# Where eleven parameter rows and five small weight loads stand in one load queue

## The chip, the cores and the metric

The kernel runs on one core of one Trainium2 chip. The time is device microseconds (us) of one execution; lower is better. A core has five engines with a queue each, and every queue is worked through in order: TensorE (PE, matrix products and transposes; PEld is its weight load), VectorE (DVE), ScalarE (ACT), GpSimd (POOL) and SyncE (SP). SP computes nothing here: it issues the transfers between HBM and the on-chip memory.

## The reference, cut to what matters

One decoder layer for 1024 prompt tokens and 64 new sample tokens (8 sequences of 8). The part around the change is the head of the layer:

```python
def rmsnorm(x, g):
    y = xf * lax.rsqrt(jnp.mean(xf * xf, axis=-1, keepdims=True) + RMS_EPS)
    return (y * g).astype(x.dtype)
...
h = rmsnorm(x, lw['g_mix'])
proj = h @ lw['w_in']                                   # 1024 x 3328
...
xs = proj + (prev - proj) * lw['mu_shift']              # token shift
r, k, v, dw, da, dg = jnp.split(xs, cuts, axis=-1)
w_log = -jax.nn.softplus(-(lw['w0'] + jnp.tanh(dw) @ lw['w2'])) - 0.5
decay = jnp.exp(-jnp.exp(w_log))
a = jax.nn.sigmoid(lw['a0'] + da @ lw['a2'])
g = jax.nn.sigmoid(dg) @ lw['g2']
```

Behind it come a recurrence over 1024 tokens (RWKV-7), a short convolution, stick-breaking attention over the prompt and over a paged cache, an output projection, a squared-ReLU MLP and a gated embedding. All of it is float32. The parameters `mu_shift`, `w0`, `a0`, `k_k`, `k_a`, `r_k`, `gn_w`, `gn_b`, `conv_w`, `g_mlp` and `g_ple` are vectors of 256 to 1024 numbers; `w2`, `a2` and `g2` are matrices of 64, 64 and 128 rows by 256.

## The kernel before

**Head of the kernel.** The 1088 tokens are nine tiles of `x`: eight of 128 rows and one of 64 rows (the sample tokens). `x_tile(i)` (L107 to L111) takes one of four buffers `xt` (`bufs=4`) and loads 128 rows of 1024 floats, 512 KB, with one transfer on SP (L110). Tile 4 therefore needs the buffer of tile 0, tile 5 that of tile 1, and so on. `gbc` (L116) is `g_mix` repeated on all partitions.

The loop over nine tiles (L181 to L202) does this for each: ACT squares the row and sums it (L189) and takes the root (L190); DVE takes the reciprocal (L192) and multiplies tile, reciprocal and `gbc` into `h` (L193), which is the last reader of the tile's buffer; PE transposes `h` in eight blocks (L198) into two of five PSUM banks that `tr()` hands out in turn; ACT copies each bank to a rounded half `h_hi` (L200) and DVE forms the remainder `h_lo` (L201). Each product of the kernel is then three matmuls: high by high, low by high, high by low.

**Weights.** `Weights.load` (L147 to L160) reads 512 KB into one of two buffers `wr` (L156), ACT rounds it to `wh` (L158), POOL forms the remainder `wl` (L159). The first one, `w_da`, is the 256 columns of `w_in` for decay, rate and gate: two transfers.

**Parameter rows.** Behind the loop, the eleven vectors are loaded as 44 rows of 128 floats into one tile `prow`, one SP transfer each (L213); PE transposes `prow` (L218), DVE copies it to `par` (L219) and forms `om`, which is one minus `mu_shift` (L221) and one minus `k_a` (L222). The transpose takes the next bank of `tr()`.

**Small weights.** `wl2` holds `w2`, `a2` and `g2`: five SP transfers (L300 to L302), 64 KB each and 128 KB for `g2`. ACT rounds it (L303), POOL forms the remainder (L304). `lora` (L344 to L353, its matmuls at L349) uses them. Then comes `sh`, the 8 rows of `state_shift` (L308), which PE transposes (L311).

**First projection.** `rw_tile` (L319 to L342) multiplies 128 columns of a weight with `h` in three chunks of 384, 384 and 320 tokens (`gemm_t`, L169 to L171), into three banks `acc()` in turn. ACT copies each bank out twice: `raw` (L330, L332) and `xs` scaled by `om` (L333); DVE adds the shifted `raw` scaled by `mu_shift` (L334). The fourth chunk needs the first bank back, and so `om`.

**What sets the order.** The program is traced in the order above, and a planner then writes each engine's queue: it steps through a model of the machine, and whenever an engine is free it gives it the earliest traced instruction that is ready in the model. So a load whose buffer isn't free yet is overtaken by later loads that need nothing. `tc.issue_after(ins)` forbids this for the instructions of its block on `ins`'s engine: they come behind `ins` in that queue. It is an order of issue only, no wait for `ins` to finish.

Of the kernel before, what the change touches and what calls it, by code (L numbers as in the profile page):

```python
# [48 lines left out]
def hybrid_step(ctx: ExitStack, tc: tile.TileContext, I, O):  # L49
    nc = tc.nc  # L50
    V, S, G, PE, SP = nc.vector, nc.scalar, nc.gpsimd, nc.tensor, nc.sync
# [46 lines left out]
    xp_in = I["x_prompt"][0]  # L98
    xs_in = I["x_sample"].rearrange("b j d -> (b j) d")
# [7 lines left out]
    def x_tile(i):  # L107
        r = 128 if i < 8 else NS
        xt = xpool.tile([128, D], F32, name="xt", bufs=4)
        SP.dma_start(xt[:r], xp_in[i * 128:i * 128 + 128, :] if i < 8 else xs_in)  # L110
        return xt, r  # L111

    xts = [x_tile(0)]
    gbc = xpool.tile([128, D], F32, name="gbc")
    gm = I["g_mix"]
    SP.dma_start(gbc, bass.AP(tensor=gm.tensor, offset=gm.offset, ap=[[0, 128], [1, D]]))  # L116
    xts += [x_tile(i) for i in range(1, 3)]


# [61 lines left out]
    for i in range(9):  # L181
        if i == 1:
            w_da = w_cols(768)
        if i + 3 < 9:
            xts.append(x_tile(i + 3))
        xt, r = xts[i]
        st = xpool.tile([128, 2], F32, name="st", bufs=5)
        h = xpool.tile([128, D], F32, name="h", bufs=3)
        S.activation(h[:r], xt[:r], AF.Square, accum_out=st[:r, 0:1])  # L189
        S.activation(st[:r, 1:2], st[:r, 0:1], AF.Sqrt, bias=eps_rms[:r], scale=1.0 / D)  # L190
        rs = xpool.tile([128, 1], F32, name="rs", bufs=5)
        V.reciprocal(rs[:r], st[:r, 1:2])  # L192
        V.scalar_tensor_tensor(h[:r], xt[:r], rs[:r], gbc[:r], op0=ALU.mult, op1=ALU.mult)  # L193
        for g in range(2):
            pt = tr().rearrange("p (k t) -> p k t", k=4)
            for k in range(4):
                c = (4 * g + k) * 128
                PE.transpose(pt[:, k, :r], h[:r, c:c + 128], ident[:r, :r])  # L198
            dst = slice(i * 128, i * 128 + r)
            S.copy(hT[0][g][:, :, dst], pt[:, :, :r])  # L200
            V.tensor_sub(hT[1][g][:, :, dst], pt[:, :, :r], f(hT[0][g][:, :, dst]))  # L201
# [6 lines left out]
    prow = consts.tile([nrows, 128], F32)  # L208
    col = {}
    at = 0  # L210
    for name, n in rows:
        src = I[name]
        SP.dma_start(prow[at:at + n, :], bass.AP(tensor=src.tensor, offset=src.offset, ap=[[128, n], [1, 128]]))  # L213
        col[name] = at
        at += n
    par = consts.tile([128, nrows], F32)
# [76 lines left out]
    def pe_tile(name, dtype=F32):  # L293
        return rp.tile([128, LW], dtype, name=name, tag="pe", bufs=12)


    wl2, wl2h, wl2l = (pe_tile(f"wl2{i}", d)[:, :768].rearrange("p (i c) -> p i c", i=3) for i, d in
                       enumerate((F32, F32R, F32R)))
    for s in range(2):
        SP.dma_start(wl2[64 * s:64 * s + 64, 0], I["w2"][0])  # L300
        SP.dma_start(wl2[64 * s:64 * s + 64, 1], I["a2"][0])
    SP.dma_start(wl2[:, 2], I["g2"][0])  # L302
    S.copy(wl2h, wl2)  # L303
    G.tensor_sub(wl2l, wl2, f(wl2h))  # L304
    shT = rp.tile([128, 8, NB], F32, name="shT")
# [71 lines left out]
    for j in range(2):  # L377
# [14 lines left out]
        for a in range(2):  # L392
            rb = pe_tile("rb", F32R)
            rbs.append((rb, rp.tile([128, 2, 64], F32R, name=f"rb8{a}")))
            for d, i0, i1 in ((rb[:, :1024], 0, 8), (rbs[a][1].rearrange("p s d -> p (s d)"), 8, 9)):
                d = d.rearrange("p (i s d) -> p i s d", i=i1 - i0, s=2)
                src = rk[:, i0:i1, :, None].to_broadcast([128, i1 - i0, 2, 64])
# [5 lines left out]
        for t0, n in CH:  # L403
            ps = tr()
            for t in range(t0, t0 + n, 128):
                r = min(128, T - t)
# [361 lines left out]
    ap = tc.alloc_tile_pool(name="att_a", bufs=1, side="right", reuse_waits="tile")  # L768
# [6 lines left out]
    for n, name in enumerate(("q_gain", "k_gain")):  # L775
        src = I[name]
# [761 lines left out]
    ap = tc.alloc_tile_pool(name="att_b", bufs=1, side="right", reuse_waits="tile")  # L1538
# [213 lines left out]
```

## Time and profile before

| | |
|---|---|
| time, median of 3 runs | 1705.01 us (1703.33 to 1708.07) |
| the profiled execution | 1706.69 us; its span, first to last instruction, 1705.1 us; so 1.6 us lie around the span |
| mean granted TensorE clock | 0.987 |
| PE busy | 1637.8 us, 96% |
| PEld / DVE / ACT / POOL busy | 87% / 65% / 48% / 43% |
| DMA | 202.26 MB, mean 119 GB/s |

In the profile each instruction has a start in us from the beginning of the span, a length, an engine (`SPq` is SP's queue, with the time that an issue took), the line in the kernel, the operation, what it writes and reads, and in square brackets how long its engine was idle before it and which instruction or transfer ended that. The word "issue" there means that the profile shows nothing waited for. The view by windows gives busy time of each engine in stretches of the span, the granted clock, the DMA engines' busy share and GB/s.

### The profile page before, as it was taken

Reading aid. Unit: us, or ns where it says so; the run is one execution under the profiler, and the core shown is the slowest. Engines: PE = TensorE matmul, PEld = TensorE weight load, DVE = VectorE, ACT = ScalarE, POOL = GpSimd, SP = SyncE. Lnnn points to the kernel's source line nnn. Section 1 sums busy time; section 2 is a strip of 40 time slices with the busy share of each in tenths; the row PEclk is TensorE's granted clock in tenths of the full one; section 3 lists DMA queues with packets and bytes.
Section 4 is the critical chain, followed back from the end, with each engine's and each line's share of the span. In section 5 each row is a group of like instructions: output and inputs, shape, how many; then the busy total and the mean of one; then the engine's idle time right before and its main releaser. Section 6 shows DMA issues by size and latency. Waiting matters only on the chain.

```text
span 1705.1 us, 30847 instructions
## 1 busy us (share of the span) xinstructions
PE 1637.8 (96%) x11853; PEld 1476.2 (87%) x11853; DVE 1105.0 (65%) x1918; ACT 820.7 (48%) x1627; POOL 727.3 (43%) x778
## 2 busy tenths in 40 slices
PE   6999899999899889999999999999999999999898
PEld 5899888889898767888887778987999999999698
DVE  6266844555277759888854345378777777764986
ACT  6633433343343657666543444364444334436753
POOL 4123121123232664443434654366655445538621
PEclk9999999999999999999999999999999999999999
DMA  5134466325523763433245665322322222323232
GB/s 189 49 120 124 142 166 178 72 78 158 160 66 96 226 170 124 137 121 116 78 121 149 187 178 189 112 84 77 97 90 87 87 87 90 98 76 105 87 120 56
DMA packets 212372, 202.26 MB, mean 119 GB/s; under 512 B 58305, under 2 KB 177761, under 8 KB 212098
## 3 DMA queue, kind: packets, MB, share of 16 engines
q1 hardware_dynamic: 202498, 179.33, 35.4%
q0 software_dynamic: 5120, 16.78, 3.3%
q10 hardware_dynamic: 4608, 4.20, 1.0%
q8 instruction: 93, 1.52, 0.4%
q14 instruction: 53, 0.43, 0.1%
HBM read 163.27 MB, written 36.98 MB: 117 GB/s over the span
## 4 chain that ended last, share of the span: by engine, by line
PE 76%; DVE 10%; DMA 6%; ACT 3%; issue 3%; SPq 2%; POOL 1%; ACTq 0%; DVEq 0%; POOLq 0%
PE b L1094 12%; PE b L1096 11%; PE b L1095 11%; PE b L1453 4%; PE b L1455 4%; PE b L1454 4%; PE b L169 3%; PE b L170 3%; PE b L171 3%; PE b L797 2%; PE b L795 2%; PE b L796 2%; PE b L942 2%; DMA wr<-in_w_in 1%; PE b L512 1%
## 5 line engine op out<-in xcount | busy, mean ns | idle before, releaser
L1075 POOL TENSOR_TENSOR wl<-wr,wh 128x512 fp32r<-128x512 f32 x182 | 255.1, 1411 | 265.5 <-ACT wh L1074 226.3
L1074 ACT CAST wh<-wr 128x512 fp32r<-128x512 f32 x308 | 187.9, 621 | 308.9 <-PE b L1095 198.0
L1522 DVE TENSOR_TENSOR x<-b,x 128x288 f32<-128x288 f32 (+1 forms) x384 | 199.2, 528 | 97.2 <-PE b L1096 86.0
L1094 PE MATMUL b<-ah,wh 128*128 128x288 f32 (+1 forms) x768 | 253.7, 331 | 3.2 <-DVE x L1522 2.1
L1096 PE MATMUL b<-ah,wl 128*128 128x288 f32 (+1 forms) x768 | 252.2, 328 | 0.0
L1095 PE MATMUL b<-al,wh 128*128 128x288 f32 (+1 forms) x768 | 252.0, 328 | 0.0
L1094 PEld LDWEIGHTS b<-ah,wh 128*128 128x128 f32 x768 | 144.5, 188 | 15.3 <-DVE x L1522 4.8
L1096 PEld LDWEIGHTS b<-ah,wl 128*128 128x128 f32 x768 | 144.5, 188 | 10.2
L1095 PEld LDWEIGHTS b<-al,wh 128*128 128x128 f32 x768 | 144.6, 188 | 9.3 <-DVE al L1426 0.3
L1094 PE MATMUL b<-nh,wh 128*128 128x512 f32 x320 | 129.1, 403 | 5.4 <-DVE x L1413 3.3
L795 PE MATMUL b<-wh,h_hi 128*128 128x256 f32 x432 | 127.4, 295 | 5.1 <-ACT sq L805 5.1
L1095 PE MATMUL b<-nl,wh 128*128 128x512 f32 x320 | 128.1, 400 | 0.0
L1096 PE MATMUL b<-nh,wl 128*128 128x512 f32 x320 | 127.7, 400 | 0.0
L797 PE MATMUL b<-wh,h_lo 128*128 128x256 f32 x432 | 126.8, 293 | 0.0
L796 PE MATMUL b<-wl,h_hi 128*128 128x256 f32 x432 | 124.7, 289 | 0.0
L1075 DVE TENSOR_TENSOR wl<-wr,wh 128x512 fp32r<-128x512 f32 x126 | 102.4, 815 | 26.4 <-ACT wh L1074 22.4
L159 POOL TENSOR_TENSOR wl<-wr,wh 128x1024 fp32r<-128x1024 f32 x26 | 64.6, 2500 | 123.0 <-ACT wh L158 118.0
L169 PE MATMUL b<-h_hi,wh 128*128 128x384 f32 (+1 forms) x336 | 115.1, 342 | 1.9 <-ACT xs L333 1.3
L170 PE MATMUL b<-h_lo,wh 128*128 128x384 f32 (+1 forms) x336 | 113.8, 339 | 0.3 <-DVE h_lo L201 0.3
L171 PE MATMUL b<-h_hi,wl 128*128 128x384 f32 (+1 forms) x336 | 112.5, 335 | 0.0
L922 DVE TENSOR_TENSOR_SCAN keep<-keep,onesq 128x128 f32<-128x128 f32 (+3 forms) x64 | 95.3, 1488 | 21.4 <-POOL keep L920 20.7
L1453 PE MATMUL b<-op,wh 128*128 128x288 f32 x320 | 95.0, 297 | 0.1
(437 smaller groups left out, 4450.6 us busy)
## 6 DMA issues: line engine op xcount, KB each, us to landing
wr<-in_w_up SPq DMA_DIRECT2D x64, 512.0 KB
wr<-in_w_down SPq DMA_DIRECT2D x64, 512.0 KB
wr<-in_w_in SPq DMA_DIRECT2D x26, 512.0 KB
wr<-in_w_out SPq DMA_DIRECT2D x16, 512.0 KB
wr<-in_w_ple_gate SPq DMA_DIRECT2D x16, 512.0 KB
xt<-in_x_prompt SPq DMA_DIRECT2D x8, 512.0 KB
stk_s<-sth ACTq DMA_DIRECT2D x32, 128.0 KB
stk_s<-stl SPq DMA_DIRECT2D x32, 128.0 KB
```

The lines of the kernel that those rows point to most:

```text
L169: PE.matmul(ps[:, :n], wh[:, k, c], a, start=(k == 0), stop=False)
L170: PE.matmul(ps[:, :n], wh[:, k, c], b, start=False, stop=False)
L171: PE.matmul(ps[:, :n], wl[:, k, c], a, start=False, stop=(k == nk - 1))
L795: PE.matmul(o, a, w[0][:, k, :], start=(k == 0), stop=False)
L797: last = PE.matmul(o, b, w[0][:, k, :], start=False, stop=(k == 7))
L1074: S.copy(h3, src)
L1075: (sub or G).tensor_sub(l3, src, f(h3))
L1094: PE.matmul(ps[:, :n], w(0, k, m), a, start=(k == 0), stop=False)
L1095: PE.matmul(ps[:, :n], w(0, k, m), b, start=False, stop=False)
L1096: PE.matmul(ps[:, :n], w(1, k, m), a, start=False, stop=(k == nk - 1))
L1453: PE.matmul(o, wh[:, k], x[:, 0, k], start=k == 0, stop=False)
L1522: V.tensor_add(p.x[:, m, t0:t0 + n], ps[:, :n], p.x[:, m, t0:t0 + n])
```

## The change

The transfers of the x tiles are kept in a list. The eleven loads of `prow` are queued on SP behind the load of tile 5, and the five loads of `wl2` behind the load of tile 8, the last. Nothing is added or removed; no size changes. `sh` and the loads of weights stay free to go anywhere.

```diff
     def x_tile(i):
         r = 128 if i < 8 else NS
         xt = xpool.tile([128, D], F32, name="xt", bufs=4)
-        SP.dma_start(xt[:r], xp_in[i * 128:i * 128 + 128, :] if i < 8 else xs_in)
+        x_dma.append(SP.dma_start(xt[:r], xp_in[i * 128:i * 128 + 128, :] if i < 8 else xs_in))
         return xt, r
 
+    x_dma = []
     xts = [x_tile(0)]
...
     for name, n in rows:
         src = I[name]
-        SP.dma_start(prow[at:at + n, :], bass.AP(tensor=src.tensor, offset=src.offset, ap=[[128, n], [1, 128]]))
+        with tc.issue_after(x_dma[5].ins):
+            SP.dma_start(prow[at:at + n, :], bass.AP(tensor=src.tensor, offset=src.offset, ap=[[128, n], [1, 128]]))
         col[name] = at
         at += n
...
-    for s in range(2):
-        SP.dma_start(wl2[64 * s:64 * s + 64, 0], I["w2"][0])
-        SP.dma_start(wl2[64 * s:64 * s + 64, 1], I["a2"][0])
-    SP.dma_start(wl2[:, 2], I["g2"][0])
+    with tc.issue_after(x_dma[8].ins):
+        for s in range(2):
+            SP.dma_start(wl2[64 * s:64 * s + 64, 0], I["w2"][0])
+            SP.dma_start(wl2[64 * s:64 * s + 64, 1], I["a2"][0])
+        SP.dma_start(wl2[:, 2], I["g2"][0])
```

## The prediction

> **What bounds the kernel now.** First the page: is one engine full?
>
> ```profile
> span 1705.1 us, 30847 instructions
> PE 1637.8 (96%) x11853; PEld 1476.2 (87%) x11853; DVE 1105.0 (65%) x1918; ACT 820.7 (48%) x1627; POOL 727.3 (43%) x778
> ```
>
> PE is, for 96%. Second, where isn't it, in the part of the span that the change touches: the view by windows, cut at marks of PE's timeline. 19.26 is where the first projection matmul starts, 39.09 where PE's last pause in the head ends.
>
> ```profile
> core 0: us, PE busy (x) PEld busy (x) DVE busy (x) ACT busy (x) POOL busy (x), PEclk, DMA share, GB/s
> 0.00:19.26 19.26, 7.46 (x32) 6.32 (x33) 11.10 (x14) 13.63 (x26) 13.64 (x41) 1.00 0.76 263
> 19.26:39.09 19.83, 16.30 (x101) 14.48 (x99) 15.45 (x27) 13.19 (x31) 5.92 (x7) 1.00 0.53 151
> 39.09:42.64 3.55, 3.55 (x11) 3.55 (x12) 1.19 (x3) 0.41 (x1) 1.09 (x2) 0.52 0.00 0
> 39.09:160.00 120.91, 120.03 (x830) 113.42 (x831) 63.03 (x82) 59.88 (x101) 32.79 (x29) 0.99 0.28 89
> 160.00:180.00 20.00, 14.90 (x96) 14.01 (x96) 13.27 (x35) 3.73 (x6) 0.00 (x0) 0.83 0.73 183
> ```
>
> From 39.09 to 160 PE is idle for 0.9 us in all, so what PE starts earlier at 39.09 it also ends earlier at 160: a gain before 39.09 is carried on, and so is a loss. Between 19.26 and 39.09 PE is idle for 19.83 - 16.30 = 3.53 us, and no other engine is full either: DVE has 4.4 us idle, ACT 6.6, and the transfers stand still for half the time. So this stretch is bound by waits. Third, SP's own timeline, the queue that the change rearranges:
>
> ```profile
> 3.44 1.08 SPq L156 DMA_DIRECT2D wr<-in_w_in  x2
> 4.56 1.46 SPq L213 DMA_DIRECT2D prow<-in_mu_shift  x1
> ...
> 10.50 0.36 SPq L110 DMA_DIRECT2D xt<-in_x_prompt  x1
> 11.93 0.23 SPq L213 DMA_DIRECT2D prow<-in_r_k  x1
> 13.38 0.23 SPq L213 DMA_DIRECT2D prow<-in_gn_w  x1
> ...
> 14.66 0.36 SPq L110 DMA_DIRECT2D xt<-in_x_prompt  x1
> ...
> 17.39 0.52 SPq L110 DMA_DIRECT2D xt<-in_x_prompt  x1
> ...
> 18.47 0.59 SPq L302 DMA_DIRECT2D wl<-in_g  x1
> 19.17 0.36 SPq L110 DMA_DIRECT2D xt<-in_x_prompt  x1
> 19.63 1.32 SPq L156 DMA_DIRECT2D wr<-in_w_in  x2
> 21.00 3.81 SPq L308 DMA_DIRECT2D sh<-in_state_shift  x1
> 24.92 0.47 SPq L110 DMA_DIRECT2D xt<-in_x_sample  x1
> SPq L213 <- DMA wr<-in_w_in: 2.2, 2, 1.2
> ```
>
> The rows of L110 from 10.50 on are x tiles 4 to 8. The last row is from SP's waits: small loads of `prow`, which depend on nothing, wait for the landing of large ones. Counted through, the two that wait for `wr` are `r_k` at 11.93 and `gn_w` at 13.38, the fourteenth and fifteenth issue; the two loads of `wr` are the sixth and seventh. So an issue here waits for the landing of the issue eight before it, and whatever is behind it in the queue waits too. Fourth, when are the buffers of the tiles free, and what does ACT wait for?
>
> ```profile
> 6.59 1.28 DVE L193 SCALAR_TENSOR_TENSOR h<-xt,rs,gbc 128x1024 f32<-128x1024 f32 x1 [0.25 <-DMA gbc<-in_g_mix]
> 9.53 1.28 DVE L193 SCALAR_TENSOR_TENSOR h<-xt,rs,gbc 128x1024 f32<-128x1024 f32 x1
> 12.12 1.28 DVE L193 SCALAR_TENSOR_TENSOR h<-xt,rs,gbc 128x1024 f32<-128x1024 f32 x1
> 14.37 3.15 DVE L193 SCALAR_TENSOR_TENSOR h<-xt,rs,gbc 128x1024 f32<-128x1024 f32 x1
> 21.21 1.28 DVE L193 SCALAR_TENSOR_TENSOR h<-xt,rs,gbc 128x1024 f32<-128x1024 f32 x1
> 18.28 1.06 ACT L189 ACTIVATE h<-xt 128x1024 f32<-128x1024 f32 x1 [0.71 <-DMA xt<-in_x_prompt]
> 21.68 1.06 ACT L189 ACTIVATE h<-xt 128x1024 f32<-128x1024 f32 x1 [0.92 <-DMA xt<-in_x_prompt]
> 23.38 0.84 ACT L303 CAST wl<-wl 128x768 fp32r<-128x768 f32 x1 [0.55 <-issue]
> 26.55 1.04 ACT L158 CAST wh<-wr 128x1024 fp32r<-128x1024 f32 x1 [2.14 <-DMA wr<-in_w_in]
> 28.82 1.08 ACT L189 ACTIVATE h<-xt 128x1024 f32<-128x1024 f32 x1
> 38.45 1.05 ACT L333 ACTIVATE xs<-b,om 128x384 f32<-128x384 f32 x2 [0.48 <-DVE h_lo L201]
> ```
>
> The five DVE rows are the last readers of tiles 0 to 4; they end at 7.87, 10.81, 13.40, 17.52 and 22.49, and from there tiles 4 to 8 could be issued. They were issued at 10.50, 14.66, 17.39, 19.17 and 24.92: 2.6, 3.9, 4.0, 1.7 and 2.4 us late. ACT waits 0.71 and 0.92 us for tiles 5 and 6. Then its queue has the cast of `wl2` and that of a later weight ahead of tile 7, and waits 0.55 and 2.14 us there, so that tile 7's square (28.82) begins long after its issue at 19.17.
>
> **The change part by part.**
>
> *The eleven `prow` loads.* They leave the places from 4.56 on. Of the free work, `sh` is then next in traced order, so I expect it behind `wr`; its 3.81 us there would end at 8.4, 0.5 us past the release of tile 4, at no cost: by the waits on `wr` (the rows at 11.93 and 13.38) what was issued up to 4.5 still lands until 13.38, and tile 4 is behind it either way. Tile 5 can go at 10.8 and not 14.66, into a hole in the transfers. It is issued 3.62 us before ACT starts on it now (14.66 to 18.28), hence lands by about 16.3 (an estimate, as it queues behind tile 4), when ACT is busy anyway: its 0.71 us go. The rows follow at 11.2. The fourth and fifth of them wait for `wr` to 13.38, where tile 6 becomes ready (13.40): I expect it at about 13.7, not 17.39, so its 0.92 us go too. Tile 7 can go at 17.6, not 19.17. Tile 8 loses the `sh` ahead of it: 22.5 or a little sooner, not 24.92. `prow` itself is issued by about 18 to 20. With the 4.29 us that tile 6 took now (17.39 to 21.68) it has landed by 24.3. What uses it and when:
>
> ```profile
> 35.46 0.26 PE L218 MATMUL b<-ident,prow 44*128 44x44 f32 x1
> 56.13 2.12 PE L349 MATMUL b<-dw,wl 128*128 128x384 f32 x6
> ```
>
> The transpose is at 35.46, 11 us behind: cost nothing, hidden by the x tiles' own chain. Without that cover every us of lateness would show one to one, since `om` gates the first `xs` at 38.45 and that the fourth chunk at 39.09.
>
> *The five `wl2` loads.* The last of them is issued at 18.47 now, between tiles 6 and 7; behind tile 8 the five take about 5 x 0.59 = 2.9 us: 23 to 26. Landing after 4.3 us is 30; the cast of 0.84 us on ACT and the remainder on POOL follow, some 33 in all, against the use at 56.13: hidden by 23 us of projection matmuls. Only a wait of ACT, whose queue is in order, can cost: queued behind a cast that waits are the casts `h_hi` of the last tiles and `xs`. I bound it from both sides: -0.55 us (the wait that ACT has on it now vanishes) and +6.6 us (the cast keeps its place at 23.38 and the load lands at 30). I take 0, near the lower end, because the planner places the cast by its own landing time, which moves with the load.
>
> *What PE gets.* PE's idle 3.53 us lie in the stretch that these tiles feed. Its work there is the fullest of the engines (16.30 us against 15.45 and 13.19), so with tiles ahead of need the stretch can't be shorter than 16.30: at most -3.5. Behind it, from 39.09 to 42.64, the granted clock is 0.52: at full clock the same matmuls take 3.55 x 0.52 = 1.85 us. If PE comes in without pauses this stretch, too, could go: at most -1.7 us. Some pauses stay, since the last tile's casts and remainders go back and forth between ACT and DVE (0.48 us is such a wait, in the row at 38.45): I leave two and a bit, 1.1 us (estimate), and count half of the slow stretch. Sum: -3.5 + 1.1 - 0.9 = **-3.3 us**. The bounds are -5.2 (all of both) and +6.6 - 2.7 (the two waits 0.55 and 2.14 that go in exchange) = +3.9.
>
> The Trainium skill (TensorE: Matmul & The Clock Gate, "The HAM clock gate") says that PE's clock falls to half after about one idle window of 3.4 us and comes back after as long a busy one. The slow stretch of 3.55 us agrees in length; by the rule it would go as a whole once no window is idle, and the sum would be -4.1 us. The pauses ahead of it are single ones of under 3.4 us, so the trace doesn't show what set it off. The same skill (DMA: Bandwidth & Descriptors, "Rules for kernel authors") advises to issue a load early and to wait for it late; by this the change is wrong for sixteen loads, and the sum would be that of rival B below. By the rows above the sixteen have 11 us and more to spare, so B stays small.
>
> The profiled execution took 1706.7 us (span 1705.1 and 1.6 around it), the sum makes 1703.4 of it. It is 1.7 us above the median of the runs, 1705.0; from the median the same sum gives **1701.7 us**.
>
> **The rivals.**
>
> *A: the tiles come earlier, and nothing comes of it.* The chain of waits has one transfer in this stretch, and it is not an x tile:
>
> ```profile
> 19.63 6.90 DMA wr<-in_w_in
> ```
>
> It is the load of the next weight, which ACT waits for at 26.55. If the planner again puts that cast ahead of tile 7, or all of `prow` ahead of tile 6 (the seventh and eighth rows wait for tiles 4 and 5, to about 16.5, so tile 6 goes no sooner than 17.4, as now), only the 0.71 us of tile 5 and some of SP's time are won. For it: nothing that the change names touches this cast. Against: it was ahead because tile 7 was late in the plan. Time: 1705.0 - 0.7 = 1704.3.
>
> *B: slower, by `wl2`.* The cast L303 stands in ACT's queue ahead of tiles 7 and 8 as it does now, and its load is issued behind tile 8. ACT then does nothing for these two tiles until `wl2` has landed. It decides from the point where `wl2` lands later than 23.4 + 2.7 us, the waits that ACT has there anyway. Price +3.9 as above; with the load held up by a full queue, as `sh` is now for 3.81 us, +7.7. Time: 1708.9 to 1712.7, middle 1710.8. For it: ACT already waits there for `wl2` (23.38) and for `wr` (26.55), so the planner takes loads for landed sooner than they are. Against: the cast moves with the load in the plan.
>
> *C: more than the window holds.* The whole order is planned anew from the first microseconds. The stage from 160 to 180 has 5.1 us of idle PE, and the first 19.26 us have 11.8. If the tiles pull the first projection's start forward or the later waits fall better, the bound of -5.2 is passed; I price it at that and a third of the 5.1: 1705.0 - 5.2 - 1.7 = 1698.1. Against: beyond 39.09 the change moves all work by the same amount, so the planner's later choices have little reason to differ.
>
> **How the numbers follow.** Forecast 0.43, A 0.25, B 0.13, C 0.19. Within 0.3% (5.1 us, about what a measurement of this kernel tells from no change) is 1699.9 to 1710.1. The forecast's own range is 1699 to 1704, and a quarter of it is below 1699.9: faster 0.11 + 0.19 = 0.30. Of B half is above 1710.1: slower 0.07. Same 0.63. The range for 8 in 10 goes from 1696.5 (past C's price) to 1707.5 (the bound +3.9 from the median is 1708.9; most of B is left out).
>
> **What would show it.** In SP's timeline: tile 5 near 10.8, tile 6 before 15, tile 7 near 17.6, tile 8 before 23, `sh` early, `wl2` last. In ACT's: no wait for tiles 5 and 6, tile 7's square before 25, the first `xs` near 35. In the windows: PE's idle time before 39 down by 2 to 3 us, and the first matmul still near 19.3. From 60 to 160 everything earlier by the same 3 us. Wrong if tile 6 is issued after 17, if ACT waits over 2 us for `wl2` or `wr`, or if the order or the idle time of PE beyond 160 us differs by more than the stretch ahead of it has won.

## The result and the profile after

| | median | lowest to highest |
|---|---|---|
| before, on the same chip | 1705.01 us | 1701.88 to 1710.14 |
| changed | 1718.49 us | 1716.65 to 1722.06 |
| ratio | 1.0075, 95% interval 1.0058 to 1.0092 | |

The change costs 13 us where 3.3 us were to be won; that is above the dearest price in the prediction, 1712.7 us. The profiled execution of the changed kernel took 1716.65 us, and its span is 9.8 us longer than that of before. The first part of its page:

```profile
span 1714.9 us, 30832 instructions
PE 1642.8 (96%) x11853; PEld 1476.6 (86%) x11853; DVE 1111.0 (65%) x1918; ACT 819.5 (48%) x1627; POOL 732.1 (43%) x778
```

The page hides the answer: the same matmuls, the same shares, 5 us more PE time and 5 us more of idle PE. So the head comes first, the part that was forecast. SP's timeline of the changed kernel (start, length of the issue):

```profile
8.00 3.25 SPq L110 DMA_DIRECT2D xt<-in_x_prompt  x2
11.30 0.37 SPq L215 DMA_DIRECT2D prow<-in_mu_shift  x1
...
13.50 0.36 SPq L110 DMA_DIRECT2D xt<-in_x_prompt  x1
...
17.59 0.35 SPq L110 DMA_DIRECT2D xt<-in_x_prompt  x1
...
18.35 0.29 SPq L215 DMA_DIRECT2D prow<-in_g_ple  x1
18.74 1.44 SPq L157 DMA_DIRECT2D wr<-in_w_in  x2
22.22 0.59 SPq L110 DMA_DIRECT2D xt<-in_x_sample  x1
...
25.39 0.58 SPq L305 DMA_DIRECT2D wl<-in_g  x1
...
27.50 0.48 SPq L311 DMA_DIRECT2D sh<-in_state_shift  x1
```

Tiles 6, 7 and 8 go at 13.50, 17.59 and 22.22 us (17.39, 19.17 and 24.92 before), `prow` is out by 18.64, `wl2` by 25.97 (25.39 and 0.58 of issue). What ACT and PE make of it, in the timeline of ACT and in that of PE:

```profile
17.44 1.09 ACT L190 ACTIVATE h<-xt 128x1024 f32<-128x1024 f32 x1
20.13 1.06 ACT L190 ACTIVATE h<-xt 128x1024 f32<-128x1024 f32 x1
23.53 1.05 ACT L159 CAST wh<-wr 128x1024 fp32r<-128x1024 f32 x1 [1.88 <-DMA wr<-in_w_in]
25.77 1.07 ACT L190 ACTIVATE h<-xt 128x1024 f32<-128x1024 f32 x1
29.94 0.85 ACT L306 CAST wl<-wl 128x768 fp32r<-128x768 f32 x1
35.84 1.07 ACT L336 ACTIVATE xs<-b,om 128x384 f32<-128x384 f32 x2
```

```profile
32.40 0.26 PE L220 MATMUL b<-ident,prow 44*128 44x44 f32 x1
51.97 2.12 PE L352 MATMUL b<-dw,wl 128*128 128x384 f32 x6
```

ACT no longer waits for tiles 5 and 6 (17.44 and 20.13), the cast of `wl2` (29.94) waits for nothing, and the first `xs` starts 2.6 us sooner. The `lora` matmuls start at 51.97, not at 56.13. Matched one by one, PE's instructions from 60 to 200 us stand 4.12 to 4.17 us earlier than in the trace of before (23 of the 982, around 175 us, 3.66). The gain was there and was carried on. Then it is lost. The median shift of PE's instructions against before, from matching the two traces:

| stretch of before (us) | 60-200 | 240-260 | 400-420 | 520-540 | 580-600 | 660-680 | 800-860 | 1100-1120 |
|---|---|---|---|---|---|---|---|---|
| after minus before (us) | -4.2 | -7.9 | -1.8 | -1.2 | +6.0 | +14.7 | +11.6 | +12.1 |

Between 200 and 800 us a median is only a rough middle, since instructions have changed places: from 240 to 260 the single shifts lie between -8.1 and +2.7. For behind 200 us the engines don't do their work in the same order. Compared position by position, 3014 of PE's 10622 queue entries, 542 of DVE's 1918, 480 of ACT's 1633, 312 of SP's 684 and 219 of POOL's 839 hold another instruction than before; apart from those of the head they all lie from about 186 to 806 us, and behind that the queues are the same again. The table's loss falls into that stretch.

What PE waits for where the loss is, in PE's timeline of the changed kernel:

```profile
585.87 0.58 PE L955 MATMUL b<-wth,vs 128*128 128x256 f32 x1 [4.53 <-DVE o L959]
587.53 0.63 PE L1098 MATMUL b<-ml,wh 128*128 128x512 f32 x1
650.76 0.50 PE L1098 MATMUL b<-nl,wh 128*128 128x512 f32 x1 [1.00 <-DVE nl L1322]
654.86 0.50 PE L1098 MATMUL b<-nl,wh 128*128 128x512 f32 x1 [1.21 <-DVE nl L1322]
666.04 0.80 PE L1097 MATMUL b<-nh,wh 128*128 128x512 f32 x1 [2.71 <-ACT rb L1364]
```

Behind the first pause the matmuls of 512 columns take 0.63 us; 0.39 is their time elsewhere. The DVE instruction `o` that ended it was late because of the one ahead of it. Timelines of DVE and then of POOL, changed kernel:

```profile
577.21 0.68 DVE L1295 TENSOR_TENSOR ml<-mixl,mh 128x512 fp32r<-128x512 f32 x1
580.91 4.58 DVE L1295 TENSOR_TENSOR ml<-mixl,mh 128x512 fp32r<-128x512 f32 x1
585.41 0.41 DVE L959 TENSOR_TENSOR o<-b,o 64x256 f32<-64x256 f32 x1
```

```profile
581.23 3.69 POOL L1078 TENSOR_TENSOR wl<-wr,wh 128x512 fp32r<-128x512 f32 x3
```

The same subtraction of 128x512 takes 0.68 us at 577.21 and 4.58 us at 580.91, where POOL's three weight remainders run beside it; it ends 0.6 us behind them. In the trace of before the planner had the `ml` ahead of such a run well apart from it:

```profile
580.94 0.68 DVE L1292 TENSOR_TENSOR ml<-mixl,mh 128x512 fp32r<-128x512 f32 x1
585.19 0.69 DVE L61 TENSOR_TENSOR wtl<-b,wth 128x512 fp32r<-128x512 f32 x1 [0.17 <-issue]
```

```profile
584.97 3.79 POOL L1075 TENSOR_TENSOR wl<-wr,wh 128x512 fp32r<-128x512 f32 x3
```

POOL's three stood 4 us later there, and beside them DVE had a subtraction from the PSUM bank `b`, which kept its 0.69 us. The windows say what these stretches are worth to PE, before and then after (span of the window, then PE busy; the clock stands third from the end):

```profile
580.00:600.00 20.00, 20.00 (x103) 17.01 (x102) 8.78 (x19) 7.44 (x17) 14.95 (x13) 1.00 0.57 171
640.00:670.00 30.00, 27.54 (x135) 22.11 (x135) 28.63 (x29) 24.30 (x45) 15.29 (x21) 1.00 0.42 135
```

```profile
580.00:600.00 20.00, 15.47 (x70) 12.71 (x70) 10.09 (x13) 6.49 (x15) 10.40 (x9) 0.83 0.46 141
640.00:670.00 30.00, 22.30 (x97) 16.66 (x97) 28.17 (x25) 20.15 (x37) 20.67 (x20) 0.94 0.37 119
```

PE stands idle for 4.5 and 7.7 us in them, where it was 0 and 2.5, and the granted clock is 0.83 and 0.94, where it was 1.00. (The counts, 70 matmuls for 103 and 97 for 135, are in part of other matmuls, since the work has shifted.)

### The profile page after: what moved, and what is told of

Its sections match the earlier page's. It is cut to its first block, busy times and chain, and to the rows that moved or that the text cites. A ratio compares the mean times of both kernels' runs of the same rounds, so it can differ in the third digit from the quotient of the medians.

```text
span 1714.9 us, 30832 instructions
## 1 busy us (share of the span) xinstructions
PE 1642.8 (96%) x11853; PEld 1476.6 (86%) x11853; DVE 1111.0 (65%) x1918; ACT 819.5 (48%) x1627; POOL 732.1 (43%) x778
## 4 chain that ended last, share of the span: by engine, by line
PE 75%; DVE 9%; DMA 6%; issue 4%; ACT 4%; SPq 1%; POOL 1%; ACTq 0%; DVEq 0%; POOLq 0%
PE b L1097 12%; PE b L1099 12%; PE b L1098 12%; PE b L1456 4%; PE b L1458 4%; PE b L1457 4%; PE b L170 2%; PE b L171 2%; PE b L172 2%; PE b L800 2%; PE b L799 2%; PE b L798 2%; PE b L945 1%; PE b L515 1%; DVE keep L925 1%
## 5 line engine op out<-in xcount | busy, mean ns | idle before, releaser
L1078 POOL TENSOR_TENSOR wl<-wr,wh 128x512 fp32r<-128x512 f32 x182 | 259.6, 1436 | 290.5 <-ACT wh L1077 242.6
```

Source lines behind the costliest of these rows:

```text
L1078: (sub or G).tensor_sub(l3, src, f(h3))
```

## The experiments

The theory: the two edits win some 3 us in the head, and lose several times as much because the planner, given a head a few us shorter, writes another order for all queues between 200 and 800 us. The rival: the two edits cost something themselves that the head doesn't show.

**Head and tail apart.** In the next kernels the order is not left to the planner. The program is planned once with the loads as before (EARLY) and once with both edits (LATE), and every queue is then chained, without waits, in an order put together from the two plans. The cut is behind the head: 32 entries of SP, 38 of ACT, 21 of DVE, 41 of POOL.

```diff
+EARLY, LATE = (None, None), (5, 8)
+HEAD, TAIL = LATE, EARLY
+CUTS = ("SP", 32), ("Activation", 38), ("DVE", 21), ("Pool", 41), ("PE", 0)
...
+    for e, n in CUTS:
...
+        order[e] = head[e][:n] + tail[e][n:]
```

> Both halves of the change, but every engine's queue behind the head is put in the order of the kernel before (each instruction queued behind its predecessor there); the head keeps the order of the changed kernel. Nothing is left out. Theory ORDER (the head gains 4.2 us, and all of the loss comes from another order that the planner chose from about 200 us on): 1705.0 - 4.2 = 1700.8, within 1699 to 1703. Rival SHIFT (the earlier head makes the later stages collide, whatever their order): 1715 to 1720. Rival LOADS (the late rows or small weights cost something later): slower than 1705, with a wait on prow or wl2 in the trace.

The other way round:

```diff
-HEAD, TAIL = LATE, EARLY
+HEAD, TAIL = EARLY, LATE
```

> Neither half of the change; the head as in the kernel before, and every queue behind it in the order of the changed kernel. Nothing is left out. ORDER: the tail's loss without the head's gain, 1718.5 + 4.2 = 1722.7, within 1719 to 1726. SHIFT or LOADS: 1705, as before, since the head isn't moved.

| ratio to before | old tail | new tail |
|---|---|---|
| old head | 1 | 1.0109 (1.0082 to 1.0135), 1723.52 us |
| new head | 0.9985 (0.9968 to 1.0001), 1702.41 us | 1.0075 (1.0058 to 1.0092), 1718.49 us |

The new head gains with either tail (0.15% and 0.34%, 2.6 and 5.8 us), the new tail loses with either head (0.90% and 1.09%, 15.3 and 18.6 us). The order of the tail is the cause. That of the head, by itself, did about what was forecast, though with the old tail the interval just reaches 1. (The chaining was not timed by itself; with the old tail the chained kernel is not slower than before.)

**One edit alone,** planned freely.

```diff
-LATE = (5, 8)
+LATE = (5, None)
```

> Only the eleven rows are queued behind tile 5; the planner is free. It gives PE and POOL the order of the kernel before from end to end (0 of PE's 10622 planned instructions stand elsewhere). ORDER: faster than before by the rows' share of the head's gain, which the SP rows put at most of it (tiles 5 to 7 come earlier by rows, only wl2's own cast and the place of sh are left): 1701 to 1704. SHIFT: slower than 1705 if the shift is over 2 us. LOADS by the rows: slower than 1705.

```diff
-LATE = (5, 8)
+LATE = (None, 8)
```

> Only the five small weight loads are queued behind tile 8; the planner is free. It gives PE, DVE, ACT and POOL the order of the changed kernel from end to end (3014 of PE's 10622 instructions at another place than before). ORDER: the tail's loss, with as much of the head's gain as these loads bring: 1717 to 1723. SHIFT: in step with the head's gain: under 1711 if the head gains less than half. LOADS by wl2: slower than 1705 and a wait on wl2 in the head.

`prow` alone: 1700.38 us, 0.9976 (0.9962 to 0.9990), the lowest median of all kernels here, faster than both given ones and a little below what was expected. Its queues of PE and POOL are those of before. `wl2` alone: 1716.65 us, 1.0065 (1.0040 to 1.0091); its queues of PE, DVE, ACT and POOL are those of the changed kernel. So one edit leaves the planner where it was and the other tips it over. A shorter head by itself doesn't do it: with `prow` alone PE stands 3.0 us earlier at 60 us in the trace, and the order stays. Neither shows a cost of its own: with `wl2` alone the `lora` matmuls, which need it, start at 52.10 us, 4 us before their time of before.

**Which part of the tail.** Both edits' head, and the new order only from 550 us on, or only up to there:

```diff
-HEAD, TAIL = LATE, EARLY
-CUTS = ("SP", 32), ("Activation", 38), ("DVE", 21), ("Pool", 41), ("PE", 0)
+HEAD, PARTS = LATE, (LATE, EARLY, LATE)
+CUTS = ("SP", (32, 371)), ("Activation", (38, 480)), ("DVE", (21, 594)), ("Pool", (41, 232)), ("PE", (0, 3690))
```

> Both halves of the change. The queues are in the order of the kernel before from the end of the head to 550 us, and in that of the changed kernel from there. Nothing is left out. If the other order costs its time where the traces part (570 to 690 us, the attention heads of the second half between output projection and norm): 1714 to 1718. If the stretch from 200 to 550 carries it: 1702 to 1706.

```diff
-HEAD, PARTS = LATE, (LATE, EARLY, LATE)
+HEAD, PARTS = LATE, (LATE, LATE, EARLY)
```

> Both halves of the change. The queues are in the order of the changed kernel to 550 us, and in that of the kernel before from there. Nothing is left out. If the loss is made behind 550 us: 1702 to 1706 (the head's gain less the 2 to 3 us that the trace of the changed kernel loses between 200 and 550). If it is made before 550: 1714 or more.

From 550 on: 1717.03 us, 1.0060 (1.0040 to 1.0079). Up to 550: 1706.88 us, 1.0003 (0.9988 to 1.0018). Against the new head with the old tail that is 0.75% (12.8 us) and 0.18% (3 us): four fifths of the loss lie behind 550 us. (1706.88 is 0.9 us above the range expected for it; the kernel before, timed beside it, was at 1706.69.)

**Is every other order bad?** Two more places for the loads, planned freely:

```diff
-LATE = (5, 8)
+LATE = (8, 8)
```

> All sixteen loads queued behind tile 8; the planner is free, and gives a third order (3611 of PE's 10622 instructions stand elsewhere than before, 3521 elsewhere than in the changed kernel). ORDER: the head gains 2 to 4 us as in the changed kernel, and the time is set by the luck of this order: anywhere from 1698 to 1720, so a result away from both 1702 and 1718 speaks for it. If instead the moved loads set the time, it is within 2 us of the changed kernel, 1718.

```diff
-LATE = (5, 8)
+LATE = (5,7)
```

> As the changed kernel, but the five small weight loads are queued behind tile 7 and not 8: one place in the queue. The planner is free and gives a fourth order (3481 of PE's 10622 instructions elsewhere than in the changed kernel). ORDER: the head's gain of 2 to 4 us and the luck of this order: 1698 to 1720. If the moved loads set the time: 1718, as the changed kernel.

1710.39 us, 1.0023 (1.0011 to 1.0034), and 1711.64 us, 1.0031 (1.0017 to 1.0045): a third and a fourth order, both worse than the old one and better than the changed kernel's. In both traces PE is again, in the median, 8 to 11 us later at 650 to 700 us than before, with a pause of 4.18 and 4.52 us at 579 and 582, this time behind a weight cast on ACT. Moving `wl2` by one tile changes the time by about 7 us, and not by way of the head: from 60 to 160 us PE is 1.2 us earlier than before in that trace, less than the 4.2 of the changed kernel, which is slower.

**The stall at 586.** The changed kernel with its own queues, and one wait: the first of POOL's three remainders waits for DVE's `ml`.

```diff
+            wl, ml = WL_BEHIND_ML
+            tc.add_manual_dep(traced[wl], ml, mybir.DependencyInfo(
+                mybir.DependencyClass.Sync, mybir.DependencyReason.DATA), reason="ml first")
```

> The changed kernel with every queue in its own order, and one wait put into it: the first of the three wl remainders on POOL (L1075 of before, 581.23 in the trace of after) waits for the ml remainder on DVE (580.91 there), which took 4.58 us beside them and 0.68 elsewhere. Theory COLLISION (the ml remainder is held up by the POOL remainders it runs beside; behind it in DVE's queue stands o, which the matmul at 585.87 waits for): ml takes about 0.7 us, PE's pause of 4.53 us before 586 is under 1.5 us and the ten matmuls behind it run at full clock (another 2 us); POOL's remainders end 0.4 us later. What is carried to the end is 4 to 6 us of after's 13: 1712.5 to 1714.5, ratio to before 1.0045 to 1.0057. Rival DEFERRED (PE lacks work there for the order's sake, whatever DVE does): another wait takes the pause's place within 30 us and the time stays at 1716.5 to 1719.

1715.53 us, 1.0062 (1.0047 to 1.0077): 0.13%, some 2 to 3 us less than the changed kernel (1.0058 to 1.0092). That is between what the two theories expect, and less than the intervals can tell apart, so the times don't show a gain. The trace tells more. DVE's, POOL's and PE's timelines of this kernel:

```profile
582.21 0.69 DVE L1299 TENSOR_TENSOR ml<-mixl,mh 128x512 fp32r<-128x512 f32 x1 [0.43 <-ACT mh L1298]
582.82 0.41 DVE L963 TENSOR_TENSOR o<-b,o 64x256 f32<-64x256 f32 x1
645.68 6.50 DVE L1326 SCALAR_TENSOR_TENSOR nl<-x,par,nh 128x512 fp32r<-128x512 f32 x4
```

```profile
582.99 3.76 POOL L1082 TENSOR_TENSOR wl<-wr,wh 128x512 fp32r<-128x512 f32 x3 [0.93 <-DVE ml L1299]
642.32 4.53 POOL L1082 TENSOR_TENSOR wl<-wr,wh 128x512 fp32r<-128x512 f32 x2
```

```profile
583.29 0.39 PE L959 MATMUL b<-wth,vs 128*128 128x256 f32 x1 [0.97 <-DVE o L963]
639.28 0.53 PE L960 MATMUL b<-wtl,vs 128*128 128x256 f32 x1 [2.46 <-DVE wtl L61]
663.02 0.61 PE L1101 MATMUL b<-nh,wh 128*128 128x512 f32 x1 [3.01 <-ACT rb L1368]
```

With the neighbours parted `ml` is back at 0.69 us, PE's pause is 0.97 us for 4.53, and its matmuls of 512 columns keep their 0.39 us. From 575 to 600 us PE goes from 1.04 us later than in the changed kernel to 4.1 us earlier: 5.1 us won on the spot, as expected. By 680 us 2.7 are left. The waits at 639 and 663 are longer than they were in the changed kernel (1.44 and 2.71), but others are shorter: from 605 to 670 PE's pauses add up to some 11.1 us in both. What is lost is pace: behind the pauses at 607 and 639 the matmuls of 512 columns take 0.63 us, some 1.5 us lost each time, and the changed kernel has one such stretch there, at 632. So the collision is shown to be the cause of that stall. That something else takes its place, as the rival has it, the trace bears out in part, and the time doesn't exclude it.

The other traces agree on the stall. All five kernels with the new order in this stretch have a pause of PE at 586 to 590 us that `o` ends: 4.53 us (changed), 3.61 (old head, new tail), 4.81 (`wl2` alone), 6.03 (new order from 550 on) and 6.00 (new order from 550 to 612, below). In the five with the old order there (before, new head with old tail, `prow` alone, new order to 550, new order from 612) no pause from 570 to 600 is ended by `o`.

**The stretch from 550 in two.** With the cuts at 612 us, the new order only in between, and only from 612 on:

```diff
+HEAD, PARTS = LATE, (LATE, EARLY, LATE, EARLY)
+CUTS = ("SP", (32, 371, 423)), ("Activation", (38, 480, 558)), ("DVE", (21, 594, 690)), ("Pool", (41, 232, 295)), ("PE", (0, 3690, 3981))
```

> Both edits, their head; the queues in the order of before but from about 550 to 612 us, where they stand in the changed kernel's. The order from 550 on costs about 12.8 us against the head with the old tail (1717.0 - 1702.4 less the part before 550). In the trace of after PE's instructions go from 1.2 us early (500 to 540) to 6 us late (580 to 600): 7.2 us, and to 11.6 late behind 740: 5.6 us. Theory TWO PLACES (each stretch of the order has stalls of its own, that add): about 1702.4 + 7.2 - 0.5 = 1709 (1707 to 1711), with the pause before 586 in the trace. Rival ONE CAUSE (the stalls of 612 to 700 only follow from the lateness at 586): 1713 or more here and no loss in the run with the new order from 612 alone.

```diff
+HEAD, PARTS = LATE, (LATE, EARLY, LATE)
+CUTS = ("SP", (32, 423)), ("Activation", (38, 558)), ("DVE", (21, 690)), ("Pool", (41, 295)), ("PE", (0, 3981))
```

> Both edits, their head; the queues in the order of before to about 612 us, and from there in the changed kernel's. Theory TWO PLACES: no pause of over 2 us at 586, but those of 640 to 667 as in the trace of after (7.7 us in six pauses against one of 1.65 in before): about 1702.4 + 5.6 = 1708 (1706 to 1710.5). Rival ONE CAUSE: 1701 to 1704, as with the old tail.

550 to 612: 1714.44 us, 1.0052 (1.0034 to 1.0070). From 612: 1709.05 us, 1.0023 (1.0011 to 1.0034). The second is as two separate places predict (1706 to 1710.5), and one cause for both falls with it. The first, at 1714.44 us, is 3 us above the range of two places and where the rival puts it: the stall repeats, larger, and the old order behind it meets a longer wait of its own than it does without (3.02 us with the new head and the old tail throughout). PE's timeline of that kernel, then DVE's:

```profile
586.79 0.58 PE L959 MATMUL b<-wth,vs 128*128 128x256 f32 x1 [6.00 <-DVE o L963]
641.20 0.80 PE L1101 MATMUL b<-nh,wh 128*128 128x512 f32 x1 [3.63 <-DVE x L1420]
```

```profile
581.86 4.55 DVE L1299 TENSOR_TENSOR ml<-mixl,mh 128x512 fp32r<-128x512 f32 x1 [1.59 <-ACT mh L1298]
```

The two parts make 0.67% and 0.38% over the new head with the old tail, together more than the 0.75% of the whole from 550: whether the first stall also makes part of what follows, as the regained 5.1 us that shrank to 2.7 suggest, or the intervals (0.2% each) make the rest, these runs don't settle.

## Why the prediction was wrong

**The step that failed** is in rival C, and the forecast leans on it without saying so: "beyond 39.09 the change moves all work by the same amount, so the planner's later choices have little reason to differ". The sum ended at 160 us and was taken to the end of the kernel from there, which holds only if the queues behind 160 us keep their order. (The prediction's last sign of being wrong, another order or other idle time beyond 160 us, is what came.) A new plan was priced on one side alone, as a further gain. The runs put -2.6 us on the head's new order with the tail kept (forecast: -3.3), and +15.3 us (1.0075 against 0.9985) on the tail's new one. Rival B had the right side, but not this mechanism: it looked for the loss in `wl2`'s landing. The trace of before already had a row that shows what a bad plan can meet: in the head, DVE's L193 at 14.37, beside two weight remainders on POOL (14.09 to 19.75), took 3.15 us for 1.28. It shows that such a pair costs, not how much: 1.9 us there, 3.9 at 580.91 in the changed kernel.

**The head, point by point.** The places of tiles 5 to 8 were right to 0.3 us, those of `prow` and `wl2` too. `sh` was wrong: it didn't go early, but last, at 27.50, at no cost. ACT's 0.71 and 0.92 us went; its wait for `wr` did not, 1.88 us at 23.53 after 2.14, and the cast still stands ahead of tile 7's square (25.77), as rival A has it. The windows of the changed kernel:

```profile
19.26:35.00 15.74, 13.82 (x86) 12.76 (x85) 13.41 (x21) 11.47 (x25) 5.74 (x4) 1.00 0.62 167
35.00:39.09 4.09, 4.08 (x32) 3.73 (x32) 3.06 (x9) 1.60 (x4) 2.33 (x5) 1.00 0.00 0
39.09:42.64 3.55, 3.55 (x25) 3.55 (x24) 0.00 (x0) 0.00 (x0) 0.00 (x0) 1.00 0.00 0
```

PE's pauses before 39.09 shrank from 3.53 to 1.93 us, less than the 2.4 of the sum. In this one execution the slow stretch from 39.09 to 42.64 was gone in full (clock 1.00, 25 matmuls for 11), worth 2.0 us, and the first chunk ran at the slow pace (0.52 us a matmul, 0.33 at full) for some three matmuls and not eight, worth 0.6. All of it together is 4.2 us; the forecast had 3.3, with more of it from pauses and half of the slow stretch. That the two numbers lie near each other is in part luck, as the next paragraph shows. `wl2` and `prow` cost nothing, as said: the cast at 29.94 and the transpose at 32.40 waited for nothing.

**How sure the head's number is.** A single trace is a poor measure of it. The `lora` matmuls, which in the old head of before start at 56.13, start in the old head of the second experiment at 53.68, and in the new head at 51.97 (changed) or 54.79 (first experiment):

```profile
53.68 2.12 PE L356 MATMUL b<-dw,wl 128*128 128x384 f32 x6
```

```profile
54.79 1.44 PE L356 MATMUL b<-dw,wl 128*128 128x384 f32 x4
```

The same queue entries in the same order differ by 2.5 and 2.8 us from one execution to the next. In the first experiment nearly all of it is slow pace, half in the first chunk and half in the second, where the window's granted clock is 0.75 with the same order that showed 1.00 in the changed kernel. In the second experiment, on balance, 0.9 us come from a transfer that landed sooner (the cast of `wr` starts at 25.67, not 26.55), and 1.6 from the slow stretch, which is gone there with the old head too (clock 1.00, 24 matmuls for 11). The windows of the first, then of the second:

```profile
39.09:42.64 3.55, 3.55 (x17) 3.55 (x17) 0.46 (x1) 0.00 (x0) 0.65 (x2) 0.75 0.00 0
39.09:42.64 3.55, 3.55 (x24) 3.55 (x23) 0.30 (x1) 0.00 (x0) 0.36 (x1) 1.00 0.00 0
```

So the slow stretch is no mark of the old order, and no part of its 2.0 us can be put down to the edits for sure. By the times, the head is worth 2.6 to 5.8 us (the two rows of the table of four). The rule that was weighed in the prediction (the Trainium skill, TensorE: Matmul & The Clock Gate, "The HAM clock gate"), by which the slow stretch goes as a whole once the pauses do, is borne out by the changed kernel's trace and not by the first experiment's, which has the same order and still shows slow matmuls there. The pauses from 19.26 to 39.09 make 1.93 us in the changed kernel, 1.94 in the first experiment and 2.29 in the second, and the stretch is slow in the first experiment alone, so the sum of these pauses doesn't decide it.

**What stays open.** One stall of the tail has its cause shown. The others are only seen: from 649 us on DVE's `nl` remainders take 6.50 us for four, beside a weight remainder, a sum and a product on POOL (3.83 for four in the trace of before, at 636.69), and the 3 us between 200 and 550 us have no place yet. Why the planner leaves its old path was not tried; that `wl2`'s place does it and `prow`'s doesn't is what the runs show.

## What to carry to other kernels

Where a planner writes the queues, a moved load is two changes: what it does at its place, and a new order for everything behind; here the second was three to six times the first and of the other sign. Before an edit in the head is priced, compare the whole queues of both programs, and where they part, keep the old order behind the edit (or try the edit's halves) before judging it. Here both edits with the old order kept came to a gain of 0.15%, at the edge of the noise. When several loads are moved together, time them one by one: the half that keeps the plan was a gain of 0.24%, the half that tips it a loss of 0.65%.

## What was unexpected of the hardware

A DVE subtraction with two operands in SBUF all but stood still beside three POOL subtractions in a row: 4.47 to 4.58 us for 0.67 in four programs, and 3.67 in a fifth (old head, new tail), each time ending some 0.6 us behind the last of the three. One that reads a PSUM bank kept its time beside the same three (the row at 585.19 of before). The Trainium skill (GPSIMD Engine Reference, "1. Specifications") says that GpSimd shares its SBUF interfaces with VectorE and that there is contention where the DVE instruction has two SBUF inputs. The rows agree. But the price isn't fixed. In the trace of before another `ml` ran beside three such subtractions (DVE's timeline, then POOL's), and it was not held to their end:

```profile
573.92 1.71 DVE L1292 TENSOR_TENSOR ml<-mixl,mh 128x512 fp32r<-128x512 f32 x1
```

```profile
573.15 5.38 POOL L1075 TENSOR_TENSOR wl<-wr,wh 128x512 fp32r<-128x512 f32 x3 [0.91 <-ACT wh L1074]
```

DVE took 1.71 us there, and it was POOL's run that grew, to 5.38 us from 3.79. So the same pair can cost DVE 1.0 us or 3.9; what decides between the two is not shown by these runs.
